# An encoder's Fourier layer, folded by its symmetries

## The chip, the core and the metric

The kernel runs on one core of a Trainium2 chip. Five engines work side by side, each with its own queue of instructions, done in order: TensorE (PE in the profile) multiplies matrices, VectorE (DVE) and ScalarE (ACT) work element by element, GpSimd (POOL) does small things and issues some DMAs, SyncE (SP) issues the others. An instruction waits for others by semaphores, and what stands behind it in its queue waits with it. The metric is the device time of one execution in microseconds (us), and the median over runs.

## The reference

Two layers over 512 positions (S) and 1024 channels (D). Layer 0 is a mixer of attention and a recurrence, layer 1 mixes by a Fourier transform. After each mixer stands a SwiGLU feed-forward network (FFN0, FFN1) with 2816 inner channels. Every part is normed before and after and added to x. The Fourier mixer is:

```python
def fourier_mixer(h, w):
    B, S, D = h.shape
    g = h.astype(jnp.float32).reshape(B, S, FOURIER_GROUPS, FOURIER_GROUP_DIM)
    f = jnp.fft.fft2(g, axes=(1, 3), norm='ortho').real
    return f.reshape(B, S, D).astype(h.dtype) @ w

# one layer
x = x + rmsnorm(mixer(rmsnorm(x, g_mix_pre)), g_mix_post)
x = x + rmsnorm(swiglu(rmsnorm(x, g_ffn_pre)), g_ffn_post)
```

Four groups of 256 channels are transformed on their own, over positions and channels, and the real part goes through a 1024x1024 map w_fourier_out.

## The kernel before

**Number format.** Every operand of a product is split into a rounded high part (hi) and the rest (lo), `split`: ACT casts hi, DVE subtracts it from the source for lo. A product is three matmuls, hi by hi, hi by lo and lo by hi (`mm3`, L108 to L111). A matmul has 128 rows of weights, 128 columns of weights and up to 512 columns of moving data.

**Weights** are streamed. `units` lists blocks of 256 rows or columns in the order of use; `prep_half` (L165) loads half a unit, 128x1024, into one of three raw buffers (NRAW = 3) by a DMA on SP and splits it into two tiles of a pool of 33 tiles of 128x1024 (`tiles`). A raw buffer is free again when its lo subtraction is done. `next_unit(ahead)` (L190) hands out the next unit and prepares some units ahead. The tile pool also holds the feed-forward's gated tiles, the transform's matrices and most intermediate values, so a tile's first writer waits for the last reader of what stood there. PSUM has 8 banks of 128x512.

**Stages** in program order: layer 0's mixer, FFN0, Fourier stage, FFN1. In the down projections and maps (`proj_tok`, L268) tokens are the rows of the output, in four tiles of 128, and the last input tiles are done token tile by token tile, so that `post_norm` (L256) and the next pre-norm of one tile run beside the matmuls of the next. `turn_x` (L246) transposes a normed token tile by PE and splits it into `hn` (hi and lo for the whole sequence, one buffer each, tags hnhi and hnlo in `hpool`). The `ffn` (L739) works on column tiles of 128 inner channels; the first unit of each FFN is done in two halves of 256 tokens (`col_tiles` with halves), so that it can begin with two token tiles turned, and the turns of the last two are deferred into its first pass.

**The Fourier stage** (L782 to L884). `pre_norm_tok` writes tokens in layer 1's pre-norm, without its gain, straight into the hn buffers: hi by ACT, lo by DVE, and calls it in FFN0's tail. The transform over positions (`pos_dft`, L829) takes 128 channels at a time: four token tiles, three products each, 512 columns of which 257 are the cosines and 255 the sines that a real transform needs: 8 x 4 x 3 = 96 matmuls. The gain is multiplied in as u is taken from PSUM (L836, by columns of `vcols`). The transform over channels (`ch_dft`, L848) makes the 256 outputs of a group in two tiles: 8 x 2 x 6 = 96 matmuls of 258 or 256 columns. `mirror` (L861) adds and subtracts cosine and sine part, and so gets tokens 0 to 256 and, reversed, 257 to 511. The map is `proj_tok` over 8 channel tiles, 4 token tiles and 2 halves of D: 8 x 4 x 2 x 3 = 192 matmuls of 512 columns, with `fin1` (post-norm, residual, pre-norm) and `turn_x` of each token tile in its tail. `load_dft` (L804) loads the four position tiles on POOL from call 32 of FFN0's hook on. `after1` (L886) writes the output of each token tile, half on SP's and half on ACT's queue.

The order within a queue follows the program text, as a scheduler places it beside the other engines. It is fixed before the kernel runs.

## Time and profile before

| What | Value |
|---|---|
| median of three runs | 1048.28 us |
| the three runs | 1048.87, 1048.28, 1046.87 us |
| the profiled execution's own time | 1047.91 us |
| its span in the trace | 1046.0 us |
| granted TensorE clock, mean | 0.994 |
| first matmul of the position transform, from the span's start | 597.17 us |
| first matmul of FFN1 | 675.81 us |

Times in the trace are counted from the span's start. The span covers the engines' instructions; the execution's own time is 1.9 us longer. Matmuls overlap: a row's duration (0.39 us for 512 columns) is longer than the distance to the next one's start, so a rate is read from starts.

The operands that the sums need besides come in rows of the engines' timelines: start, duration, engine and line, operation, output and inputs, shape, and in brackets how long the engine stood idle before it and whose instruction ended that.

### The profile page before, as it was taken

Reading aid. Unit: us, or ns where it says so; the run is one execution under the profiler, and the core shown is the slowest. Engines: PE = TensorE matmul, PEld = TensorE weight load, DVE = VectorE, ACT = ScalarE, POOL = GpSimd, SP = SyncE. Lnnn points to the kernel's source line nnn. Section 1 sums busy time; section 2 is a strip of 40 time slices with the busy share of each in tenths; the row PEclk is TensorE's granted clock in tenths of the full one; section 3 lists DMA queues with packets and bytes.
Section 4 is the critical chain, followed back from the end, with each engine's and each line's share of the span. In section 5 each row is a group of like instructions: output and inputs, shape, how many; then the busy total and the mean of one; then the engine's idle time right before and its main releaser. Section 6 shows DMA issues by size and latency. Waiting matters only on the chain.

```text
span 1046.0 us, 12311 instructions
## 1 busy us (share of the span) xinstructions
PE 1030.3 (99%) x4959; PEld 857.9 (82%) x4959; DVE 479.3 (46%) x735; ACT 381.9 (37%) x629; POOL 68.2 (7%) x82
## 2 busy tenths in 40 slices
PE   8999998999999999999999999999999999999997
PEld 7887776789888888888888888898888888888885
DVE  6869988664532222323333555644232232234304
ACT  5378567634432112322322454334211132233202
POOL 1056010110000000000100100100000000000000
PEclk8999999999999999999999999999999999999999
DMA  6434213403734322232442023026432223224002
GB/s 224 125 95 151 67 41 102 141 1 95 224 90 134 103 81 81 93 109 81 142 155 66 21 81 122 17 85 201 124 118 81 81 81 124 78 81 141 1 1 81
DMA packets 72981, 102.41 MB, mean 98 GB/s; under 512 B 3878, under 2 KB 61275, under 8 KB 72924
## 3 DMA queue, kind: packets, MB, share of 16 engines
q1 hardware_dynamic: 69722, 92.44, 28.5%
q0 software_dynamic: 2624, 8.13, 2.4%
q10 hardware_dynamic: 578, 1.05, 0.3%
q8 instruction: 39, 0.64, 0.3%
q14 instruction: 18, 0.15, 0.0%
HBM read 99.51 MB, written 2.10 MB: 97 GB/s over the span
## 4 chain that ended last, share of the span: by engine, by line
PE 89%; DVE 7%; ACT 2%; issue 1%; DMA 1%; POOL 1%; SPq 0%; DVEq 0%; POOLq 0%; ACTq 0%
PE pc L109 15%; PE pc L110 15%; PE pc L111 15%; PE pj L111 10%; PE pj L110 10%; PE pj L109 10%; DVE p L582 2%; DVE wlo L106 1%; DVE p L588 1%; PE pv L111 1%; PE pT L251 1%; PE pv L110 1%; PE pv L109 1%; DVE aT L106 1%; PE pqk L109 1%
## 5 line engine op out<-in xcount | busy, mean ns | idle before, releaser
L106 DVE TENSOR_TENSOR wlo<-raw,whi 128x1024 fp32r<-128x1024 f32 x170 | 206.7, 1239 | 271.2 <-ACT whi L103 220.1
L110 PE MATMUL pc<-hnlo,whi 128*128 128x512 f32 (+1 forms) x768 | 285.1, 372 | 0.0
L109 PE MATMUL pc<-hnhi,whi 128*128 128x512 f32 (+1 forms) x768 | 284.6, 372 | 0.5 <-ACT hnhi L103 0.5
L111 PE MATMUL pc<-hnhi,wlo 128*128 128x512 f32 (+1 forms) x768 | 284.9, 371 | 0.0
L103 ACT CAST whi<-raw 128x1024 fp32r<-128x1024 f32 x164 | 167.7, 1049 | 118.1 <-PE pj L110 31.0
L110 PEld LDWEIGHTS pc<-hnlo,whi 128*128 128x128 f32 x768 | 144.7, 188 | 25.5 <-DVE hnlo L106 0.4
L109 PEld LDWEIGHTS pc<-hnhi,whi 128*128 128x128 f32 x768 | 144.2, 188 | 25.7 <-ACT hnhi L103 1.0
L111 PEld LDWEIGHTS pc<-hnhi,wlo 128*128 128x128 f32 x768 | 144.6, 188 | 25.0
L109 PE MATMUL pj<-whi,gs 128*128 128x512 f32 x352 | 136.9, 389 | 0.0
L110 PE MATMUL pj<-wlo,gs 128*128 128x512 f32 x352 | 136.9, 389 | 0.0
L111 PE MATMUL pj<-whi,gs 128*128 128x512 f32 x352 | 136.9, 389 | 0.0
L93 ACT ACTIVATE gated<-pc 128x512 f32<-128x512 f32 x44 | 26.2, 597 | 271.6 <-PE pc L111 271.6
L749 DVE TENSOR_TENSOR gated<-gated,pc 128x512 f32<-128x512 f32 x44 | 30.2, 686 | 112.8 <-PE pc L111 112.8
L109 PEld LDWEIGHTS pj<-whi,gs 128*128 128x128 f32 x352 | 66.1, 188 | 13.8
L110 PEld LDWEIGHTS pj<-wlo,gs 128*128 128x128 f32 x352 | 66.1, 188 | 13.8
L111 PEld LDWEIGHTS pj<-whi,gs 128*128 128x128 f32 x352 | 66.1, 188 | 13.5
L262 ACT ACTIVATE junk<-pj 128x512 f32<-128x512 f32 x32 | 19.2, 599 | 94.8 <-DVE y L261 57.7
L217 POOL TENSOR_TENSOR r<-m,mhalf 128x1 f32<-128x1 f32 x32 | 17.5, 546 | 543.3 <-DVE m L216 536.8
L261 DVE TENSOR_TENSOR y<-pj,gpost 128x512 f32<-128x512 f32 x32 | 21.9, 688 | 56.6 <-PE pj L111 56.5
L103 ACT CAST gs<-gated 128x512 fp32r<-128x512 f32 x44 | 25.3, 618 | 52.1 <-PE pj L110 32.2
L106 DVE TENSOR_TENSOR gs<-gated,gs 128x512 fp32r<-128x512 f32 x44 | 28.4, 686 | 31.3 <-ACT gs L103 31.3
L93 ACT ACTIVATE p<-p,mn 128x512 f32<-128x512 f32 x32 | 23.0, 720 | 25.8 <-DVE mn L582 24.3
(192 smaller groups left out, 1221.9 us busy)
## 6 DMA issues: line engine op xcount, KB each, us to landing
raw<-in_w_ffn_gate_dram SPq DMA_DIRECT2D x44, 512.0 KB, 4.1
raw<-in_w_ffn_up_dram SPq DMA_DIRECT2D x44, 512.0 KB, 4.8
raw<-in_w_ffn_down_dram SPq DMA_DIRECT2D x44, 512.0 KB, 3.7
raw<-in_w_in_dram SPq DMA_DIRECT2D x20, 512.0 KB, 4.6
raw<-in_w_mix_out_dram SPq DMA_DIRECT2D x8, 512.0 KB, 3.4
raw<-in_w_fourier_out_dram SPq DMA_DIRECT2D x8, 512.0 KB, 3.8
pos<-in_dft_pos_dram POOLq DMA_DIRECT2D x8, 256.0 KB, 5.7
bias<-in_alibi_dram POOLq DMA_DIRECT2D x4, 448.0 KB, 5.3
```

The source lines that it names most:

```text
L93: ins = A.activation(out_, in_, func, **kw)
L103: A.copy(hi, src)
L106: lo_eng.tensor_tensor(out=lo, in0=src, in1=f(hi), op=ALU.subtract)
L109: T.matmul(ps, lhsT=l[0], rhs=r[0], start=start, stop=False)
L110: T.matmul(ps, lhsT=l[0], rhs=r[1], start=False, stop=False)
L111: T.matmul(ps, lhsT=l[1], rhs=r[0], start=False, stop=stop)
L217: G.tensor_tensor(out=r, in0=m, in1=mhalf[:, 0:1], op=ALU.pow)
L251: T.transpose(pt[:, k * P:(k + 1) * P], xh[:, k * P:(k + 1) * P], ident)
L261: V.tensor_tensor(out=ys[h], in0=ps[h], in1=g[:, h * S:(h + 1) * S], op=ALU.mult)
L262: A.activation(junk, ps[h], AF.Square, scale=RD, accum_out=ss[h])
L582: last_score[0] = V.tensor_tensor_reduce(out=pr[m], in0=ps[m], in1=bias[h][:, 384 - t * P:384 - t * P + S], op0=ALU.add, op1=ALU.min, scal ...
L749: V.tensor_tensor(out=gated[fc], in0=gated[fc], in1=ps, op=ALU.mult)
```

## The change

The transform is folded by its symmetries. Cosines over a group's 256 channels are even about channel 128, sines odd. So the pre-norm multiplies by the gain first (h), then adds and subtracts the mirrored channels (j and 256 - j): w holds four groups of 128 sums, with channel 0 in place, and four of 128 differences. `pos_dft` computes the cosines of the sums (258 columns) and the sines of the differences (256): 4 groups x 4 token tiles x 2 x 3 matmuls. Channel 128 of every group is gathered apart by `pos_rest`, 12 matmuls of 258 columns with every fourth column as weights. `ch_dft` needs only output channels 0 to 127: 4 groups x 8 matmuls, and `ch_rest` makes output channel 128 of every group, the rest's rows and the sums for token 256, in 10.

Since outputs k and 256 - k of a group have the same even part and the opposite odd part, the map's rows are folded too: `fold_w` loads rows j (SP) and 256 - j (an indirect DMA on POOL), adds and subtracts on DVE, and writes both back to a DRAM tensor `wfold` (POOL), one group after each of FFN0's units 0 to 3. The map's four units are loaded from there; `last_unit` keeps the prefetch from reaching them until FFN0 is through. The lo parts of the first two (units 48 and 49, LO_POOL) are subtracted on POOL instead of DVE.

The even part `fe` and the odd part `fo` of the transform, and the rows beside them, stand in the hn buffers (`feo`, `rows_`), where the normed tokens stood. The map runs over 256 positions in two halves i = 1 and i = 0 of 128, even and odd into banks of their own: 96 matmuls and 8 more of `map_rest`. Token 256 needs sums over channels by e256 (DVE: four tiles of wfold loaded again, times a column each, added up in `acc`, and split). `map_out` takes difference and sum of the two: tokens t and 512 - t, then the norms. The token tiles 1 and 2 are in reversed order from here on: their x comes by indirect gathers from a DRAM copy `scratch` that SP wrote in FFN0's tail, and goes to the output by indirect scatters on POOL in `after1`. `row_index` makes the index columns on POOL at the kernel's start (eight of iota and memset each).

Both token tiles of i = 1 are turned after the whole map. The other two are deferred into FFN1's first pass, which covers the first three weight units (six column tiles) in halves, and two more column tiles in whole width from then on (`wide`). `load_ch` builds the small channel matrices on POOL, mostly by memsets and one-column DMAs, at hook call 8; the position matrices come in pieces with a few POOL instructions each.

```diff
-LO_POOL = ()
+LO_POOL = (48, 49)
...
-        units.append(unit_rows(w_fourier_out, u * 256))
+        units.append(unit_rows(wfold, u * 256))
...
+    def fold_w(g):
+        a, b, c = (tile1k("fold") for _ in range(3))
+        nc.sync.dma_start(a, w_fourier_out[g * 256:g * 256 + P, :])
+        gather(b, w_fourier_out, rowx["w%d" % g])
+        G.memset(b[0:1, :], 0.0)
+        V.tensor_tensor(out=c, in0=a, in1=b, op=ALU.add)
+        V.tensor_tensor(out=a, in0=a, in1=b, op=ALU.subtract)
+        for z, w in enumerate((c, a)):
+            G.dma_start(wfold[g * 256 + z * P:g * 256 + (z + 1) * P, :], w)
...
-        while emitted[0] <= i + ahead and emitted[0] < len(units):
+        while emitted[0] <= i + ahead and emitted[0] < last_unit[0]:
...
-                    if deferred and (h == 1 or c == P):
+                    if deferred and (h == 1 or c == P) and not (late and h == 0):
                         deferred.pop(0)()
+                while late and deferred:
+                    deferred.pop(0)()
...
+            ug, uu, vg = next_unit(2), next_unit(1), next_unit(0)
+            col_tiles([(ug, 0), (ug, P), (uu, 0), (uu, P), (vg, 0), (vg, P)],
+                      lambda i, ps: consume(i, ps, 0) if i < 4 else consume(i - 4, ps, 1), True, True)
+            vu = next_unit(3)
+            col_tiles([(vu, 0), (vu, P)], lambda i, ps: consume(i + 2, ps, 1), False)
...
+        h = tile1k("h")
+        V.tensor_tensor(out=h, in0=xt[t], in1=g_pre1[0], op=ALU.mult)
+        hv = h.rearrange("p (g c) -> p g c", c=256)
+        w = tile1k("w")
+        wv = w.rearrange("p (z g c) -> p z g c", g=4, c=P)
+        V.tensor_copy(wv[:, :, :, 0:1].rearrange("p z g c -> p g (z c)"), hv[:, :, 0:256:P])
+        V.tensor_tensor(out=wv[:, 0, :, 1:P], in0=hv[:, :, 1:P], in1=hv[:, :, 255:P:-1], op=ALU.add)
+        V.tensor_tensor(out=wv[:, 1, :, 1:P], in0=hv[:, :, 1:P], in1=hv[:, :, 255:P:-1], op=ALU.subtract)
         hi = hn["hi"][:, 2 * t:2 * t + 2, :].rearrange("p a b -> p (a b)")
         lo = hn["lo"][:, 2 * t:2 * t + 2, :].rearrange("p a b -> p (a b)")
+        for z in range(2):
+            sl = slice(z * S, (z + 1) * S)
+            A.activation(hi[:, sl], w[:, sl], AF.Copy, scale=r)
+            V.scalar_tensor_tensor(out=lo[:, sl], in0=w[:, sl], scalar=r, in1=f(hi[:, sl]), op0=ALU.mult, op1=ALU.subtract)
...
+        if t >= 2:
+            nc.sync.dma_start(scratch[(t - 2) * P:(t - 1) * P, :], xt[t])
...
+        w128 = tile1k("w128")
+        G.memset(w128, 0.0)
+        for q in range(3):
+            G.dma_start(w128[32 * q:32 * q + 4, :], w_fourier_out.rearrange("(g j) d -> g j d", j=256)[:, P, :])
...
+                G.dma_start(w[:, 0:257], dft_pos[z, k * P:(k + 1) * P, 0:257])
+                G.dma_start(w[:, 258:513], dft_pos[z, k * P:(k + 1) * P, 257:512])
+                G.memset(f(w[:, 257:258]), 0.0)
...
+    ffn(0, after0, 6, load_dft, early=lambda u: fold_w(u - 1) if 0 < u < 5 else None)
+    last_unit[0] = len(units)
+    load_last()
+    prep_one()
...
+            for z, (r0, o0, n) in enumerate(((0, 0, 258), (257, 256, 256))):
+                o = (z * 4 + g) * P
+                mm3(ps[:, o0:o0 + n], [a[:, o:o + P] for a in hf[t]], [a[:, r0:r0 + n] for a in posT[t]],
+                    t == 0 and z == 0, t == 3 and z == 1, skip_group_check=True)
...
+            mm3(ps[:, 0:258], [a[:, S:2 * S:4] for a in hf[t]],
+                [a[:, 0:258] for a in posT[t]], t == 0, t == 3)
...
+    for g in range(4):
+        pos_dft(g, (0, 1, 2))
+    pos_rest((0, 1, 2))
+    pos_rest((3,))
+    uts["r"] = pair("u", F32R)
+    split(*[a[:, 0:258] for a in uts["r"]], ups["r"][:, 0:258])
+    for g in range(4):
+        pos_dft(g, (3,))
+        take_u(g)
...
+    feo = hpool.tile([P, 16, 256], F32R, name=nm("feo"), tag="hnhi")
+    rows_ = hpool.tile([P, 4, D], F32R, name=nm("rows"), tag="hnlo")
+    acch, accl, wr, fr = rows_[:, 0, :], rows_[:, 1, :], rows_[:, 2, :], rows_[:, 3, 0:256]
...
+        ut, ur = uts[g], uts["r"]
+        mm3(pe[:, 0:258], (chw(0), chw(1)), [a[:, 0:258] for a in ut], True, False)
+        for a in ur:
+            T.matmul(pe[:, 0:258], lhsT=chw(4 + g), rhs=a[:, 0:258], start=False, stop=a is ur[1])
+        mm3(po[:, 0:256], (chw(2), chw(3)), [a[:, 256:512] for a in ut], True, True)
+        eo = feo[:, 4 * g:4 * g + 4, :]
+        e, o = fe[g], fo[g] = (eo[:, 0, :], eo[:, 1, :]), (eo[:, 2, :], eo[:, 3, :])
+        split(*e, pe[:, 0:256])
...
+        A.copy(wr, w128)
+        V.tensor_tensor(out=wr[32:64, :], in0=w128[32:64, :], in1=f(wr[32:64, :]), op=ALU.subtract)
...
+    gather(xr[1], scratch, rowx["d"])
+    gather(xr[2], scratch, rowx["c"])
...
+    for g in range(4):
+        raw = raws.tile([P, 1024], F32, name=nm("raw"), tag="raw")
+        nc.sync.dma_start(raw, wfold[g * 256:g * 256 + P, :])
+        if g:
+            V.scalar_tensor_tensor(out=acc, in0=raw, scalar=e256[g], in1=acc, op0=ALU.mult, op1=ALU.add)
+        else:
+            V.tensor_scalar(out=acc, in0=raw, scalar1=e256[0], scalar2=None, op0=ALU.mult)
+    V.scalar_tensor_tensor(out=acc[0:32, :], in0=w128[0:32, :], scalar=e256["r"][0:32, :], in1=acc[0:32, :], op0=ALU.mult, op1=ALU.add)
+    split(acch, accl, acc)
...
+        ps = psm[i]
+        mm3(ps[0][h], [a[:, sl] for a in fe[g]], [a[:, d] for a in wf[g][0]], g == 0, False)
+        mm3(ps[1][h], [a[:, sl] for a in fo[g]], [a[:, d] for a in wf[g][1]], g == 0, g == 3 and i == 1)
...
+        for h in range(2):
+            A.copy(ts[h], psm[i][1][h])
+        for z in (0, 1) if i else (1, 0):
+            for h in range(2):
+                V.tensor_tensor(out=ys[h], in0=psm[i][0][h], in1=ts[h], op=ALU.add if z else ALU.subtract)
+            t = (3 - z, z)[i]
+            post_norm(t, ys, g_post1)
+            pre_norm(t, g_fpre1)
+            ys = ts
...
+    for i in (1, 0):
+        for g in range(4):
+            for h in range(2):
+                map_part(i, h, g)
+        for h in range(2):
+            map_rest(i, h)
+        prep_one()
+        if i == 0:
+            new_hn()
+            turn_x(0)
+            turn_x(1)
+        map_out(i)
+    deferred.extend((lambda: turn_x(2), lambda: turn_x(3)))
...
+        if t in (1, 2):
+            G.indirect_dma_start(out=out, out_offset=rowx[("od", "oc")[t - 1]], in_=xt[t], in_offset=None)
+            return
...
-    ffn(1, after1, 4)
+            q.dma_start(out[r:r + P, h * S:(h + 1) * S], xt[t][:, h * S:(h + 1) * S])
+    ffn(1, after1, 4, wide=True)
```

Three places in the queues show where the change moves instructions. On POOL, from the end of FFN0's tail on, r is the root of a norm, ch the channel matrices, w_810 the tile with row 128 of each group of the map (w128), x_817 and x_818 the reversed token tiles. Before:

```order
L217 TENSOR_TENSOR r_4750<-m_4749,mhalf 128x1
L819 DMA ch_4769<-in_dft_ch_dram 128x1024
L217 TENSOR_TENSOR r_4763<-m_4762,mhalf 128x1
L819 DMA ch_4771<-in_dft_ch_dram 128x1024
L217 TENSOR_TENSOR r_5232<-m_5231,mhalf 128x1
```

And now:

```order
L251 TENSOR_TENSOR r_4910<-m_4909,mhalf 128x1
L888 MEMSET w_810_4925 128x1024
L199 DMA x_817_4942<-scratch,ixd 128x1024
L890 DMA w_810_4925<-in_w_fourier_out_dram 4x1024 x3
L107 TENSOR_TENSOR wlo_4933<-raw_4930,whi_4932 128x1024
L987 MEMSET feo_5084 128x1 x8
L199 DMA x_818_4943<-scratch,ixc 128x1024
L107 TENSOR_TENSOR wlo_4939<-raw_4936,whi_4938 128x1024
L107 TENSOR_TENSOR wlo_5075<-raw_5072,whi_5074 128x1024
L107 TENSOR_TENSOR wlo_5081<-raw_5078,whi_5080 128x1024
L251 TENSOR_TENSOR r_5306<-m_5305,mhalf 128x1
```

Between the last root of FFN0 and the first of the Fourier stage POOL had one channel matrix to load; now a memset, two gathers, three DMAs, eight small memsets and four lo subtractions stand there. These four are called A, B, C and D below, and the gathers d and c.

On ACT, at the start of the Fourier stage, put is a bank of the position transform, u its split value. Before:

```order
L788 ACTIVATE hnhi_4562<-x_82,r_4763 128x1024
L836 ACTIVATE u_4836<-put_4773,vcols 128x512
L836 ACTIVATE u_4842<-put_4783,vcols 128x512
L836 ACTIVATE u_4848<-put_4793,vcols 128x512
L836 ACTIVATE u_4854<-put_4803,vcols 128x512
```

And now:

```order
L846 ACTIVATE hnhi_4688<-w_4916,r_4910 128x512 x2
L104 CAST whi_4938<-raw_4936 128x1024
L991 CAST rows_5085<-w_810_4925 128x1024
L104 CAST u_5033<-put_5020 128x258
L104 CAST u_5042<-put_4944 128x512
L104 CAST u_5051<-put_4963 128x512
```

The first cast of u stood right behind the last token; the cast of a weight and that of these rows 128, which come by POOL's DMAs, stand between them now.

On DVE, from the last map weights to the first norm behind the map, y is a half of a token tile on its way to the post-norm, pj and pm are the map's banks. Before:

```order
L106 TENSOR_TENSOR wlo_5166<-raw_5163,whi_5165 128x1024
L106 TENSOR_TENSOR wlo_5172<-raw_5169,whi_5171 128x1024
L106 TENSOR_TENSOR wlo_5184<-raw_5181,whi_5183 128x1024
L106 TENSOR_TENSOR wlo_5190<-raw_5187,whi_5189 128x1024
L261 TENSOR_TENSOR y_5223<-pj_5107,gpost_5101 128x512
```

And now:

```order
L107 TENSOR_TENSOR wlo_5196<-raw_5193,whi_5195 128x1024
L1002 TENSOR_TENSOR rows_5085<-pe_5160,rows_5085 64x256
L107 TENSOR_TENSOR wlo_5202<-raw_5199,whi_5201 128x1024
L1029 TENSOR_SCALAR acc_5205<-raw_5206,e_839_5098 128x1024
L1027 SCALAR_TENSOR_TENSOR acc_5205<-raw_5209,e_842_5116,acc_5205 128x1024
L1027 SCALAR_TENSOR_TENSOR acc_5205<-raw_5212,e_845_5134,acc_5205 128x1024
L1027 SCALAR_TENSOR_TENSOR acc_5205<-raw_5215,e_848_5152,acc_5205 128x1024
L1030 SCALAR_TENSOR_TENSOR acc_5205<-w_810_4925,e_850_5171,acc_5205 32x1024
L107 TENSOR_TENSOR wlo_5282<-raw_5279,whi_5281 128x1024
L107 TENSOR_TENSOR rows_5085<-acc_5205,rows_5085 128x1024
L107 TENSOR_TENSOR wlo_5288<-raw_5285,whi_5287 128x1024
L1057 TENSOR_TENSOR y_5292<-pm_5225,yt_5291 128x512
```

The first value that DVE takes from a map bank stood behind four lo subtractions; it now also stands behind the four products with re-loaded tiles (raw_5206 to raw_5215) and acc's split, with FFN1's first weights (wlo_5282, wlo_5288) between them.

201 lines of the change are left out of this document (125 added, 76 removed).

## The prediction

> **What bounds the kernel now.** I read the page from its top: span, busy times, and the chain of work that ended last.
>
> ```profile
> span 1046.0 us, 12311 instructions
> PE 1030.3 (99%) x4959; PEld 857.9 (82%) x4959; DVE 479.3 (46%) x735; ACT 381.9 (37%) x629; POOL 68.2 (7%) x82
> PE 89%; DVE 7%; ACT 2%; issue 1%; DMA 1%; POOL 1%; SPq 0%; DVEq 0%; POOLq 0%; ACTq 0%
> ```
>
> PE carries 89% of the chain, so on the whole fewer matmuls mean less time. The change shortens one stage, and that stage is what counts. The PE timeline gives its borders (start, duration, instruction), and the view by windows its rate.
>
> ```profile
> 597.17 0.39 PE L109 MATMUL put<-pos,hnhi 128*128 128x512 f32 x1
> ...
> 613.49 0.28 PE L109 MATMUL pe<-u,ch 128*128 128x258 f32 x1
> ...
> 630.48 0.40 PE L109 MATMUL pj<-whi,f 128*128 128x512 f32 x1
> ...
> 675.81 0.28 PE L109 MATMUL pc<-hnhi,whi 128*128 128x256 f32 x1
> ...
> 689.46 0.74 PE L109 MATMUL pc<-hnhi,whi 128*128 128x256 f32 x4 [0.24 <-ACT hnhi L103]
> ```
> ```profile
> core 0: us, PE busy (x) PEld busy (x) DVE busy (x) ACT busy (x) POOL busy (x), PEclk, DMA share, GB/s
> 597.17:613.49 16.32, 16.32 (x74) 13.51 (x72) 6.40 (x12) 6.43 (x12) 2.76 (x5) 1.00 0.30 97
> 613.49:616.36 2.87, 2.87 (x26) 2.87 (x24) 2.47 (x5) 2.01 (x5) 0.00 (x0) 1.00 0.00 0
> 630.48:647.06 16.58, 16.58 (x76) 13.71 (x75) 10.30 (x16) 8.05 (x14) 0.00 (x0) 1.00 0.57 178
> ```
>
> The Fourier stage runs from the first position matmul (597.17, called t = 0 from here on) to FFN1's first matmul (675.81): 78.64 us. In its first two windows PE is busy all the time at a granted clock of 1.00. The weight loads count the matmuls that started: 72 of 512 columns in 16.32 us, **0.227 us** each; 24 of 256 or 258 in 2.87 us, **0.120 us** each. So a matmul of half the columns costs about half, and cutting columns pays. No other engine is near its limit here: DVE is busy 10.30 of the 16.58 us of the last window.
>
> **PE's own gain.** Before, the stage has 96 position and 192 map matmuls of 512 columns (288 x 0.227 = 65.3 us), 96 channel matmuls of half size (11.5) and 16 transposes (1.6): 78.4, against 78.64 in the trace. After, it has 96 + 12 position, 32 + 10 channel matmuls of half size (150 x 0.120 = 18.0) and 104 of the map (23.6): 41.6 us without transposes. PE drops some 35 us of work. FFN1 then turns two more column tiles to halves: 96 x 0.120 = 11.5 instead of 48 x 0.227 = 10.9, **+0.6 us**. The weight fold, the token fold and the gathers lie on DVE, SP and POOL, outside PE.
>
> **What is late next.** What used to hide under 78 us of PE must now fit under 42, in the order that the queues have been given. I added durations of rows along these queues.
>
> The first two rows give shortest, median and longest of eight, in ns; the others count, busy time and mean of a group, and then size and median landing of a DMA.
>
> ```profile
> L494 POOL TENSOR_TENSOR gate<-gate,xc x8: 1287/1296/2266, 59.9 to 74.6; 128x512 f32<-128x512 f32 x8
> L520 POOL TENSOR_TENSOR gate<-gate,th x8: 1282/1785/2917, 86.4 to 99.8; 128x512 f32<-128x512 f32 x8
> ```
> ```profile
> L819 POOL DMA_DIRECT2D ch<-in_dft_ch_dram x2 | 1.1, 572 | 0.0
> ...
> masks.py:197 POOL MEMSET ident<- 128x128 f32 x1 | 0.2, 204 | 0.3 <-POOLq L935 0.3
> ```
> ```profile
> L106 DVE TENSOR_TENSOR wlo<-raw,whi 128x1024 fp32r<-128x1024 f32 x170 | 206.7, 1239 | 271.2 <-ACT whi L103 220.1
> ...
> L103 ACT CAST whi<-raw 128x1024 fp32r<-128x1024 f32 x164 | 167.7, 1049 | 118.1 <-PE pj L110 31.0
> ...
> raw<-in_w_fourier_out_dram SPq DMA_DIRECT2D x8, 512.0 KB, 3.8
> ```
> ```profile
> raw<-in_w_ffn_gate_dram SPq DMA_DIRECT2D x44, 512.0 KB, 4.1
> ...
> out_dram<-x SPq DMA_DIRECT2D x4, 256.0 KB, 2.0
> ```
>
> *POOL queue.* At t = 6.8 it is through with the last token's root and a vector load; SP's write of the last token tile to the scratch, issued at 4.4, lands a microsecond later. Then come a memset of 128x1024 (about 1.0, an estimate between the 0.204 of 128x128 and eight times it), the gather of token tile d, three small DMAs (3 x 0.57), and the lo subtraction A; eight tiny memsets (0.3); the gather of c; the subtractions B, C and D, each 128x1024. No row shows a gather's issue: a plain DMA takes 0.57 of POOL, the longest POOL instruction of the page's groups here is 2.92. I take 1.3 for each, nearer to the plain DMA, which moves the same 512 KB; the upper end, 5.8, is that longest row doubled for 128x1024. A subtraction of 128x512 takes 1.29 at best, 1.79 in the median of the crowded group, 2.92 at worst, so 128x1024 lies between 2.6 and 5.8. I take **2.9**, near twice the uncrowded row, since most of DVE's work at this time reads one operand from PSUM. POOL then ends D at 6.8 + 1.0 + 1.3 + 1.7 + 0.3 + 1.3 + 4 x 2.9 = **24.0**.
>
> [...]
>
> *Raw buffers.* There are three, so the load of a raw tile waits for the lo subtraction three tiles back. D frees the buffer that the first half of the last map unit waits for: issued 24.1, landed 27.9 (3.8), cast 1.05, lo 1.24: 30.2. The four re-loads of folded tiles for acc go through the same buffers: the second can be issued only at 30.3 and lands at 34.1; three products and the 32-row one follow (34.1 + 4 x 1.3 = 39.4). FFN1's first weights stand behind them: loaded at 39.5, cast to 40.6, lo 41.9; acc's lo 43.0, another weight's lo **44.2**. Only then does DVE's queue reach the differences of map half 1, whose banks PE finished at about 34.
>
> *Token chain.* One token of post-norm and pre-norm:
>
> ```profile
> 649.75 0.69 DVE L261 TENSOR_TENSOR y<-pj,gpost 128x512 f32<-128x512 f32 x1 [3.39 <-PE pj L111]
> 651.50 0.56 POOL L217 TENSOR_TENSOR r<-m,mhalf 128x1 f32<-128x1 f32 x1 [48.17 <-DVE m L216]
> 652.10 1.42 DVE L266 SCALAR_TENSOR_TENSOR x<-y,r,x 128x512 f32<-128x512 f32 x2 [0.69 <-POOL r L217]
> ...
> 655.20 1.41 DVE L243 SCALAR_TENSOR_TENSOR xn<-x,r,gpre 128x512 f32<-128x512 f32 x2
> ```
>
> 649.75 to 656.61 is 6.9 us. With two differences ahead (1.4) the first token is done at 44.2 + 1.4 + 6.9, about 52.7; the second, with two weights' lo subtractions queued between, 7.6 later at 60.3. PE turns it, ACT casts it (0.54), and FFN1's first matmul starts at **60.9**. PE needs its map until about 46.5 (it starts the map at 21.0 and loses 1.4 to a bank that a cast in ACT's queue frees late), so 14 us of idle PE are left before FFN1. Against 78.64 this is **-17.7 us**: half of what PE saves. From D's end to FFN1 it is 36.9 us in single file; a microsecond on POOL is a microsecond of the end.
>
> *Start of the stage.* ACT's queue has the cast of the map's rows 128 (w128) ahead of every u cast. Their DMAs stand behind the gather (the last issued at 10.3 and landed at 12.6: 2.3, a little over the 2.0 of 256 KB), so the cast ends at 14.2 and the first channel matmul waits from 13.0 to 15.0, with 1.0 more behind DVE's lo of these rows. These 3 us lie within the 60.9 and add nothing to it.
>
> *FFN0's tail.* The 33-tile pool now also holds two channel tiles, h and w there, so weight casts wait for PE to let tiles go. A wait of this kind shows cast and lo (1.05 + 1.24) less six matmuls (1.36), 0.93; I count three of them, **+2.8 us**, between 0 (the tiles come free in time) and 5.
>
> *FFN1's start.* Its first pass now covers six column tiles, whose third unit's weights are cast behind the token chain, and the last two turns come together.
>
> ```profile
> 688.82 1.08 ACT L103 CAST hnhi<-pT 128x512 fp32r<-128x512 f32 x2 [5.54 <-PE pT L251]
> 689.44 1.29 DVE L106 TENSOR_TENSOR hnlo<-pT,hnhi 128x512 fp32r<-128x512 f32 x2 [5.23 <-ACT hnhi L103]
> ```
>
> Before, PE lost 0.24 and a second gap of about 0.5 here. Now PE has nothing beside four pairs of these pieces: 1.0 until the first hi, 0.8 until the last lo, and 1.6 for the third unit: 3.4, so **+2.6 us** (0 if the tokens are early, 5 if they are late).
>
> *The end.* Token tiles 1 and 2 go out by POOL scatter, and the last plain output waits for them.
>
> ```profile
> 1035.22 0.54 POOL L217 TENSOR_TENSOR r<-m,mhalf 128x1 f32<-128x1 f32 x1 [4.89 <-DVE m L216]
> 1040.66 0.54 POOL L217 TENSOR_TENSOR r<-m,mhalf 128x1 f32<-128x1 f32 x1 [4.90 <-DVE m L216]
> ...
> 1041.24 1.41 DVE L266 SCALAR_TENSOR_TENSOR x<-y,r,x 128x512 f32<-128x512 f32 x2 [0.72 <-POOL r L217]
> ...
> 1042.68 0.34 ACTq L888 DMA_DIRECT2D out_dram<-x  x1
> ```
>
> The scatter of tile 2 starts at about 1035.22 + 0.54 + 0.06 + 1.41 + 0.7 = 1037.9; with 1.3 of issue and a landing of 4.1 as for other 512 KB it is done at 1043.3, past the 1042.68 at which the last write was issued: **+1 us** (0.5 to 2).
>
> **The sum**: -17.7 + 0.6 + 2.8 + 2.6 + 1.0 = -10.7. The profiled execution's own time is 1047.91 (0.37 below the median of the three runs), so 1037.2; I round to **1038**.
>
> **The rivals.**
> *More of the gain arrives.* If subtractions take 2.6 (1.2 saved in all), gathers 0.57 (1.5) and the three loads in the single file 3.3 each (1.5), and the FFN0 term is 0 (2.8), the net is -10.7 - 7.0 = -17.7. A stage bound by PE alone would give -35 + 0.6, and some 6 back for the last token's chain: -28. Between the two, about 1026 (1020 to 1032). For it speaks that DVE and ACT have room (46% and 37%); against it the three raw buffers.
> *POOL and DVE get in each other's way.* With 5.1 per subtraction (4 x 2.2 = +9) the net is about -2: 1046. The 2917 in the gate row speaks for it, the median of 1296 against it. In this case the work on POOL takes back nearly everything.
> *Slower: the gathers hold POOL.* If an indirect DMA of 128 rows takes G of POOL's time, the two in the middle cost 2 x (G - 1.3), since everything behind D is in single file; at the end the scatter of tile 2 stands ahead of the last token's root, which it delays from G = 2.8 on, and the landing moves by G - 1.3 too. G = 3 gives 5.4 in all (-5), G = 5 gives 7.4 + 6.0 = 13.4, so +2.7: **1050.5**. It turns the sign at about 4.3. The 0.57 of plain DMAs speaks against it; that no indirect DMA is in the trace leaves it open.
> *The half-size matmuls don't get cheap* (strided weights, sums of mixed widths in one bank): 150 at 0.227 instead of 0.120 is +16 of PE, and with none of it under waits -10.7 + 16 = +5.3, 1053. The second window speaks against it.
>
> **How the numbers follow.** The forecast (1033 to 1044) gets 0.54, more of the gain 0.18, POOL against DVE 0.13, the gathers 0.11, full-price matmuls 0.04. The range goes from 1026, half of the gain's case, to 1049, past the contention and its edge: 0.54 + 0.09 + 0.13 + 0.04 from the gathers' lower half, 0.80. This kernel's measurements tell differences from about 0.2% (2.1 us) on. Slower by that (over 1050.4) takes most of the gathers' and the full-price cases, 0.13; within it the edges of both and of the contention, 0.08; faster 0.79.
>
> **What would show it.** PE's timeline: 41 to 43 us of matmul time from the first position matmul to the last of the map, and an idle stretch of 10 to 18 us before FFN1's first matmul, which starts 57 to 64 us after t = 0. POOL: four subtractions of 2.6 to 3.5, gathers of 1 to 2. The chain: DVE, SP's loads and POOL in the stage instead of PE. Waits of raw loads ended by POOL. I am wrong if that idle stretch is under 5 us, if a gather or a subtraction is above 4, or if FFN0's end moves by more than 5.

## The result and the profile after

| | before | after |
|---|---|---|
| median of four runs | 1047.82 us (1046.87 to 1048.87) | **1040.60 us** (1040.22 to 1042.30) |
| ratio after to before, with its 95% interval | | 0.9934 (0.9917 to 0.9951) |
| the profiled execution's own time | 1047.91 us | 1040.47 us |
| its span | 1046.0 us | 1038.7 us |

The kernel is 7.2 us faster, where some 10 were forecast (the terms add up to -10.7, the time was rounded up), and the time lies in the range. The page of the kernel after, from the lines that were shown of before:

```profile
span 1038.7 us, 12339 instructions
PE 1004.3 (97%) x4877; PEld 836.9 (81%) x4877; DVE 497.4 (48%) x761; ACT 377.8 (36%) x621; POOL 123.7 (12%) x200
PE 77%; DVE 11%; issue 4%; POOL 3%; ACT 3%; DMA 2%; DVEq 0%; POOLq 0%; ACTq 0%
```

PE works 26 us less (1030.3 to 1004.3), and its share of the chain falls from 89% to 77%: what it no longer does was replaced in the chain, for the greater part, by DVE, POOL and DMA. The PE timeline of the kernel after (start, duration, instruction, idle time ahead and what ended it) has the borders of the terms, and what is new among its waits:

```profile
531.98 0.50 PE L110 MATMUL pj<-whi,gs 128*128 128x512 f32 x1 [0.48 <-ACT gs L104]
544.20 0.50 PE L110 MATMUL pj<-whi,gs 128*128 128x512 f32 x1 [1.02 <-ACT gs L104]
556.03 0.50 PE L110 MATMUL pj<-whi,gs 128*128 128x512 f32 x1 [0.48 <-ACT gs L104]
...
616.98 0.39 PE L110 MATMUL pe<-u,ch 128*128 128x258 f32 x1 [2.56 <-ACT u L104]
...
619.88 0.58 PE L110 MATMUL po<-u,ch 128*128 128x256 f32 x1 [2.03 <-DVE u L107]
...
627.37 0.40 PE L110 MATMUL pm<-whi,feo 128*128 128x512 f32 x1
...
654.27 1.29 PE L285 MATMUL pT<-ident,xn 128*128 128x128 f32 x8 [3.11 <-DVE xn L277]
661.78 1.97 PE L285 MATMUL pT<-ident,xn 128*128 128x128 f32 x8 [6.22 <-DVE xn L277]
663.57 1.01 PE L110 MATMUL pc<-hnhi,whi 128*128 128x256 f32 x3
```

The first position matmul (t = 0) starts at 599.71, the map's first at 27.7 and its last pair at 50.8 from there, and FFN1's first matmul at 663.57, which is t = 63.86. PE idles 3.11 and then 6.22 us for the token chain (DVE's xn), and the eight transposes that follow take 1.29 and 1.97 us. The same borders in both traces measure the terms of the sum:

| Term | forecast | before | after | measured |
|---|---|---|---|---|
| FFN0's tail: start of t = 0 | +2.8 | 597.17 | 599.71 | +2.54 |
| stage: t = 0 to FFN1's first matmul | -17.7 | 78.64 | 63.86 | **-14.78** |
| FFN1's first to last matmul (the +0.6 and +2.6) | +3.2 | 362.60 | 365.97 | +3.37 |
| last matmul's start to the span's end | +1.0 | 7.59 | 9.16 | +1.57 |
| sum | -10.7 | 1046.0 | 1038.7 | -7.30 |

Only one term is off by more than a microsecond; that some of the others came right by luck is said further down. The chain of waits in the stage (start, duration, engine or DMA) shows where it went; the rows are those from the last two subtractions on POOL to the first difference, without the pieces of under half a microsecond:

```profile
619.41 4.72 POOL wlo L107 x2
624.14 4.21 DMA raw<-wfold
628.38 1.06 ACT whi L104
629.46 1.24 DVE wlo L107
630.71 3.94 DMA raw<-wfold
634.75 1.30 DVE acc L1027
636.06 5.00 DMA raw<-in_w_ffn_gate_dram
641.44 1.06 ACT whi L104
642.53 1.19 DVE wlo L107
643.71 1.07 DVE rows L107
646.05 1.29 DVE y L1057 x2
```

This is the single file that the prediction drew up, in its order: D on POOL, the raw buffer it frees, the last map weights, the second re-load for acc, FFN1's first weights, acc's split, the difference. D ended at 624.12 (t = 24.4; 24.0 forecast). The three loads took 4.21 + 3.94 + 5.00 = 13.15 us where the prediction had 3.8 for each of the first two and, by its times, 4.1 for the third (issued behind the product at 34.1 + 1.3, loaded at 39.5). The first difference came at t = 46.3 instead of 44.2. What POOL's instructions cost (count and shape, busy time, mean in ns, idle time ahead), grouped from t = 0 on to the map's middle:

```profile
L107 POOL TENSOR_TENSOR wlo<-raw,whi 128x1024 fp32r<-128x1024 f32 x4 | 9.5, 2384 | 1.2 <-ACT whi L104 1.1
...
L199 POOL DMA_INDIRECT x<-scratch,ixd x1 | 1.4, 1412 | 0.2 <-issue 0.2
L199 POOL DMA_INDIRECT x<-scratch,ixc x1 | 1.0, 1019 | 0.2 <-issue 0.2
```

A gather holds POOL for 1.41 and 1.02 us (1.3 forecast), so the rival in which it takes over 4 falls. A subtraction takes 2.38 (2.9 forecast), so 4 x 0.5 were gained there. They were given back, and 0.4 more: POOL idles 1.1 us ahead of C for a cast that stands behind u's casts in ACT's queue, and the last token's root, ahead of all this, ends at t = 8.2 instead of 6.8.

### The profile page after: what moved, and what is told of

It is laid out like the page before. It is cut to its first block, busy times and chain, and to the rows that moved or that the text cites. A ratio compares the mean times of both kernels' runs of the same rounds, so it can differ in the third digit from the quotient of the medians.

```text
span 1038.7 us, 12339 instructions
## 1 busy us (share of the span) xinstructions
PE 1004.3 (97%) x4877; PEld 836.9 (81%) x4877; DVE 497.4 (48%) x761; ACT 377.8 (36%) x621; POOL 123.7 (12%) x200
## 4 chain that ended last, share of the span: by engine, by line
PE 77%; DVE 11%; issue 4%; POOL 3%; ACT 3%; DMA 2%; DVEq 0%; POOLq 0%; ACTq 0%
PE pc L110 15%; PE pc L112 15%; PE pc L111 15%; PE pj L110 8%; PE pj L112 8%; PE pj L111 8%; DVE wlo L107 2%; DVE p L617 2%; DVE p L623 1%; DVE x L300 1%; POOL wlo L107 1%; DMA raw<-wfold 1%; POOL r L251 1%; DVE aT L107 1%; PE pqk L110 1%
## 5 line engine op out<-in xcount | busy, mean ns | idle before, releaser
L107 DVE TENSOR_TENSOR wlo<-raw,whi 128x1024 fp32r<-128x1024 f32 x166 | 202.2, 1240 | 233.7 <-ACT whi L104 182.2
L110 PE MATMUL pc<-hnhi,whi 128*128 128x512 f32 (+1 forms) x784 | 288.2, 369 | 1.0 <-ACT hnhi L104 1.0
L112 PE MATMUL pc<-hnhi,wlo 128*128 128x512 f32 (+1 forms) x784 | 288.3, 368 | 0.5 <-DVE wlo L107 0.5
L111 PE MATMUL pc<-hnlo,whi 128*128 128x512 f32 (+1 forms) x784 | 288.4, 368 | 0.0
L112 PEld LDWEIGHTS pc<-hnhi,wlo 128*128 128x128 f32 x784 | 148.3, 189 | 25.5 <-DVE wlo L107 1.0
L110 PEld LDWEIGHTS pc<-hnhi,whi 128*128 128x128 f32 x784 | 148.0, 189 | 25.8 <-ACT hnhi L104 1.7
L111 PEld LDWEIGHTS pc<-hnlo,whi 128*128 128x128 f32 x784 | 148.3, 189 | 24.6 <-DVE hnlo L107 0.2
L111 PEld LDWEIGHTS pj<-wlo,gs 128*128 128x128 f32 x352 | 66.1, 188 | 13.7
L296 ACT ACTIVATE junk<-pj 128x512 f32<-128x512 f32 x24 | 14.3, 597 | 74.5 <-DVE y L295 53.4
L295 DVE TENSOR_TENSOR y<-pj,gpost 128x512 f32<-128x512 f32 x24 | 16.4, 687 | 48.1 <-PE pj L112 48.1
```

What stands on the lines that cost most here:

```text
L107: lo_eng.tensor_tensor(out=lo, in0=src, in1=f(hi), op=ALU.subtract)
L110: T.matmul(ps, lhsT=l[0], rhs=r[0], start=start, stop=False, **kw)
L111: T.matmul(ps, lhsT=l[0], rhs=r[1], start=False, stop=False, **kw)
L112: T.matmul(ps, lhsT=l[1], rhs=r[0], start=False, stop=stop, **kw)
L295: V.tensor_tensor(out=ys[h], in0=ps[h], in1=g[:, h * S:(h + 1) * S], op=ALU.mult)
L296: A.activation(junk, ps[h], AF.Square, scale=RD, accum_out=ss[h])
```

## The experiments

Each is the kernel after with one edit, unless said otherwise, and each ratio is to the kernel before. The theory was the prediction's, corrected by the trace: the end is set by the single file, POOL's subtractions and the four re-loads. Against it stood the start of the stage (casts in ACT's order), the low clock (0.50 in after from 619.88 to 625.37 us), the tile pool and the outputs.

### Without the sums for token 256 (e1)

```diff
-    acc = tile1k("acc")
-    for g in range(4):
-        raw = raws.tile([P, 1024], F32, name=nm("raw"), tag="raw")
-        nc.sync.dma_start(raw, wfold[g * 256:g * 256 + P, :])
...
-    split(acch, accl, acc)
...
-            for a in (acch, accl):
-                T.matmul(psm[i][1][h], lhsT=chw(13), rhs=a[:, d], start=False, stop=a is accl)
+            T.matmul(psm[i][1][h], lhsT=chw(13), rhs=wr[:, d], start=False, stop=True)
```

It leaves out the sums of the four groups for token 256.

> Leaves out the sums for token 256 from the four folded groups (the four re-loads of wfold, the products on DVE and acc's split); the two matmuls that added acc are one with the w128 rows. Single-file theory: DVE's queue reaches the first difference of map half 1 when PE is through with that half and ACT has copied two banks, about 40.4 us after the first position matmul instead of 46.3; the 17.5 us from there to FFN1's first matmul stay: FFN1 starts at 58 instead of 63.9, the time is about 1034.6. Rival (PE's late start and its low clock set the end): the time falls by less than 2 us.

1035.94 us, ratio 0.9891 (0.9875 to 0.9908): 4.7 us faster than after. FFN1's first matmul comes at t = 55.38, 8.5 us earlier, so the products and re-loads were in the file; but FFN1 then takes 368.76, 2.8 more than after. Two waits on its PE timeline that after does not have:

```profile
656.85 1.18 PE L110 MATMUL pc<-hnhi,whi 128*128 128x256 f32 x3 [0.69 <-DVE hnlo L107]
...
671.63 0.39 PE L110 MATMUL pc<-hnhi,whi 128*128 128x256 f32 x1 [1.31 <-ACT whi L104]
```

PE waits for the lo part of the turned tokens and for the hi part of a weight: when the stage is shorter, the next things that are late are FFN1's tokens and weights.

### The sums on PE (e2)

Token 256's row is made by matmuls with one column of weights, 26 in all, in the map's second half, so that nothing is loaded again.

```diff
-        e256[g] = sm("e256")
-        V.tensor_copy(e256[g], pe[:, 256:257])
+        e256[g] = [small.tile([P, 1], F32R, name=nm("e256"), tag="e%d" % i, bufs=5) for i in range(2)]
+        split(*e256[g], pe[:, 256:257])
...
+            for g in range(4):
+                mm3(row, e256[g], [a[:, d] for a in wf[g][0]], False, False, skip_group_check=True)
+            T.matmul(row, lhsT=e256["r"], rhs=wr[:, d], start=False, stop=False, skip_group_check=True)
```

> The same sums for token 256 by 26 matmuls with one weight column each on PE, in place of re-loads, products and split. Single-file theory: PE works 5.9 - 0.9 = 5 us longer in a stretch where it was idle for over 10, its map ends at about 56, DVE's file is 6 us shorter: FFN1 starts at 58 to 59, the time is about 1035.5. Rival (PE is what the stage waits for): 5 us of PE work cost up to 5, 1041 to 1045.

1036.23 us, ratio 0.9896 (0.9879 to 0.9912): 4.4 us faster. The map's last matmul comes at t = 55.7 instead of 50.8, later by the new matmuls, and still FFN1 starts at 58.44, 5.4 earlier. PE has no idle stretch left between map and FFN1 that is longer than 0.4 us. Against e1, which has neither the re-loads nor these matmuls, FFN1 starts 3.1 later but then takes 366.24 instead of 368.76, so in the time the added matmuls cost 0.3 us, which is within the runs' spread.

### The lo parts back on DVE (e3)

```diff
-LO_POOL = (48, 49)
+LO_POOL = ()
```

> The four lo subtractions A to D on DVE instead of POOL. Single-file theory: DVE idles from 610.1 to 616.2 in the trace and takes 1.24 for each instead of 2.38, so D is done some 4 us earlier and the chain behind it (load, cast, lo, re-load) moves with it; DVE gets 5 us more work, most of it before: FFN1 starts 3 us earlier (1 to 5), the time is about 1037.5. Rival (DVE is the bound of the stage and the move to POOL is what makes the gain): slower by 2 to 5, 1043 to 1046.

1037.97 us, ratio 0.9915 (0.9898 to 0.9931): 2.6 us faster. FFN1 starts at t = 58.62 (-5.2) and takes 367.62 (+1.65). A subtraction takes 1.24 on DVE, which stood idle in after for 6.05 us ahead of 616.19, and 2.38 on POOL behind gathers and waits. The two waits at the start of the stage go too (the map begins at t = 20.5 instead of 27.7), but e4, below, shows that this alone is worth nothing. This part of the change costs time.

### The casts of u ahead of the rows' cast (e4)

```diff
+        u_casts.append(A.copy(uts[g][0], ups[g]))
...
-        A.copy(wr, w128)
+        order_after(A.copy(wr, w128), u_casts)
```

> The cast of the w128 rows is ordered behind the casts of u on ACT. Single-file theory: the two waits of 2.6 and 2.0 us before the channel matmuls go, PE's clock stays full there and the channel stage ends some 7 us earlier, but only the 1.1 us that POOL waits for a cast lies in the file: FFN1 starts 1 us earlier (0 to 2), the time is about 1039.5. Rival (PE's late start and its low clock set the end): 4 to 7 us faster, 1034 to 1036.5.

1040.80 us, ratio 0.9937 (0.9920 to 0.9953): nothing gained. Yet the start of the stage is as it was meant. Windows of this kernel (start and end, length, busy time of PE, weight loads, DVE, ACT, POOL, clock, DMA share, GB/s):

```profile
599.95:614.50 14.55, 14.55 (x110) 14.55 (x109) 9.45 (x18) 8.46 (x17) 8.96 (x10) 1.00 0.45 149
614.50:618.00 3.50, 3.50 (x32) 3.50 (x31) 1.90 (x5) 1.84 (x4) 3.33 (x11) 1.00 0.69 183
```

PE goes from the position into the channel matmuls without a wait, at a clock of 1.00, and the map begins at t = 20.1 instead of 27.7. FFN1 begins at 64.02 all the same. D ends at t = 23.3, 1.1 us earlier, but the chain of this kernel goes from C, at t = 21.0, through a raw load of 6.44 us, and has its first difference at t = 46.4 as after has at 46.3. The 1 us that was expected did not come. So the 7.5 us at the start lay beside the file, as the prediction had it of its 3 us.

### Channel matrices late, and plain outputs (e5)

```diff
-        if calls[0] == 8:
+        if calls[0] == 31:
             load_ch()
...
-            G.indirect_dma_start(out=out, out_offset=rowx[("od", "oc")[t - 1]], in_=xt[t], in_offset=None)
-            return
-        r = (P, None, None, 0)[t]
+        r = (P, 3 * P, 2 * P, 0)[t]
```

Rows of the output of two token tiles stay in reversed order.

> Two edits at two places that the trace keeps apart. The channel matrices are loaded at hook call 31 instead of 8, so two tiles of the pool come free in FFN0's down projection; and token tiles 1 and 2 are written by plain DMAs (in reversed order of rows, so the output differs there). Tile theory: the three waits of PE for a gs cast (0.5, 1.0, 0.5) go and the first position matmul starts at 597.2 to 597.7 instead of 599.7. End theory: from the last matmul to the end of the span 7.6 us instead of 9.2. Together 3.5 us: about 1037. Rivals: the waits come from the fold's work on DVE and POOL, then 599.7 stays; the end is that of the last plain write, then 9.2 stays.

1039.89 us, ratio 0.9935 (0.9918 to 0.9952). FFN0's three waits are still 0.48, 1.02 and 0.48, so it isn't the time at which the channel matrices take their tiles. The end takes 8.92 instead of 9.16: the scatters aren't the 1.57 us. Neither of the two theories held.

### PE kept busy ahead of the turns (e6)

```diff
-            turn_x(0)
-            turn_x(1)
+            for n, t in ((13, 0), (26, 1)):
+                w_ = bank("pT")
+                for _ in range(n):
+                    T.matmul(w_, lhsT=chw(0), rhs=wf[0][0][0][:, 0:S], start=True, stop=True)
+                turn_x(t)
```

> 39 more matmuls of 512 columns into the banks of the transposes, 13 before the first turn and 26 before the second, where PE is idle: they are overwritten, and only keep PE busy. Single-file theory: the transposes and the first FFN1 matmuls run at full clock, but PE waits less early and more later, for the third unit's weights and the last tokens: FFN1 starts up to 1 us earlier, the time changes by less than 1, 1040 to 1041. Clock rival: the two slow stretches cost what they show, 0.9 in the transposes and 1.3 in FFN1's first 22 us: 1038.4.

1043.96 us, ratio 0.9970 (0.9959 to 0.9982): 3.4 us slower than after, which neither forecast had. Its PE timeline at the turns:

```profile
655.17 1.03 PE L285 MATMUL pT<-ident,xn 128*128 128x128 f32 x8
...
661.96 1.03 PE L285 MATMUL pT<-ident,xn 128*128 128x128 f32 x8
...
666.21 0.74 PE L110 MATMUL pc<-hnhi,whi 128*128 128x256 f32 x4 [3.22 <-ACT hnhi L104]
```

The transposes take less now (1.03 instead of 1.29 and 1.97; the granted clock is 1.00 from 651 to 664 us, where after has 0.71 from 650.90 to 663.57), and the second set is 1.2 us earlier counted from t = 0. But then ACT's cast is late, by 3.22 us: it stands behind a piece of the next token's norm in ACT's queue here, and ahead of it in after. And t = 0 itself is 1.35 later than in after, which it already was when FFN0's down projection began (478.01 against 476.68), far ahead of the edit. Whether the clock alone is worth anything can't be read from this run: it moved the wait and the start together.

### FFN1's first pass as before (e7)

```diff
-    ffn(1, after1, 4, wide=True)
+    ffn(1, after1, 4)
```

> FFN1's first pass covers one unit pair (four column tiles) in halves as before, with the turns of the last two tokens inside it. Theory: the last tokens are ready only at about 674 and 680, so PE waits for them twice, some 4 us in all, and saves 0.6 of half-size matmuls and the wait for the third unit: 2 to 4 us slower, 1042.5 to 1044.5. Rival (the wide pass costs the 2.6 us that the forecast gave it): 1 to 3 us faster, 1037.5 to 1039.5.

1040.26 us, ratio 0.9936 (0.9919 to 0.9952). FFN1 takes 366.00 against 365.97, and neither of the two forecasts came. Of the 4 us of waits for the last tokens the timeline shows 1.10 and 0.24. The pass over six column tiles neither costs nor saves in the balance: what FFN1 loses, it loses with the old pass as well. The +0.6 and +2.6 of the sum came out right together, but not as the price of that pass.

### The three of e2, e3 and e4 together (e8)

The row for token 256 on PE, the lo parts on DVE and the casts of u first.

> The row for token 256 on PE, the lo subtractions on DVE and the w128 cast behind the casts of u, together. Theory: with the file gone, map half 1 is taken as PE finishes it (about 32.5 after the first position matmul), 17.5 us later FFN1 starts at 50 to 53 instead of 63.9; 3 to 4 us of that are given back in FFN1's first pass to weights and tokens that are late: about 1032 (1030 to 1034). Rival (two of the three shorten the same wait, so the gains don't add): no better than the best alone, 1035 to 1036.5.

**1031.01 us**, ratio 0.9847 (0.9830 to 0.9863): 9.6 us faster than after, more than the 4.4, 2.6 and 0 of the three alone, and faster than both kernels. The PE timeline around the end of its map:

```profile
649.66 1.91 PE L285 MATMUL pT<-ident,xn 128*128 128x128 f32 x16
651.91 0.50 PE L110 MATMUL pc<-hnhi,whi 128*128 128x256 f32 x2 [0.34 <-ACT hnhi L104]
...
653.68 0.39 PE L110 MATMUL pc<-hnhi,whi 128*128 128x256 f32 x1 [1.27 <-DVE hnlo L107]
```

FFN1 starts at t = 51.96, 0.34 us after the turns, and PE was busy for 50.9 of the 52 us. The file is gone; PE bounds the stage again. FFN1 takes 368.25, so 2.3 us of what the stage wins are lost there.

### The fold in two other buffers (e9), the prefetch free (e11)

Both start from e8, and both were to find what FFN0 waits for. e9 takes the fold's three tiles out of the pool of 33 (the first two lines below); e11 lets the prefetch reach the map's units in FFN0 (the last).

```diff
-        a, b, c = (tile1k("fold") for _ in range(3))
+        a, b = (xpool.tile([P, D], F32, name=nm("fold"), tag="x2" if z else "x3") for z in range(2))
...
-    last_unit[0] = len(units) - 4 - NF // 2 * 3
```

> e8 with the fold's tiles taken from the two buffers that later hold the reversed tokens, not from the pool: a + b replaces b, and 2a - (a + b) replaces a. Rotation theory: the pool hands out its 33 buffers in turn, and the twelve tiles of the fold shift which buffer a weight or gs tile gets; without them the three waits of PE for gs in FFN0 (0.5, 1.0, 0.5) go, the first position matmul starts at 597.3 instead of 599.9 and the time is 1028.6. Rival (the waits come from the fold's work on DVE, POOL and SP): 599.5 to 600.5, and 1031.

> e8 without the line that keeps the prefetch from the map's units until FFN0 is through: four halves of them are loaded and cast in FFN0's tail, as in the kernel before. Hold-back theory: the three waits of PE for gs in FFN0 come from the order that this line makes, they go, the first position matmul starts at 597.5 to 598 instead of 600, and the time is 1028 to 1029.5. Rival (the waits come from which pool buffers are taken, and the map's first weights were not waited for): 599.5 to 600.5, and within 1 us of 1031.

e9: 1069.14 us, ratio 1.0211 (1.0197 to 1.0225), which neither forecast had. The two buffers are those of token tiles 2 and 3, which FFN0 still uses, so the whole fold moved behind FFN0's tail. The trace shows it there:

```profile
632.02 0.58 PE L110 MATMUL pe<-u,ch 128*128 128x258 f32 x1 [12.69 <-ACT u L953]
```

FFN1 starts at t = 89.99, 38.0 us later than in e8. So much does the fold of the weights cost when it runs behind FFN0, with two buffers and one group after another. FFN0's three waits are 0.48, 1.02 and 0.48 in this kernel too, without any fold beside them.

e11: 1040.19 us, ratio 0.9931 (0.9914 to 0.9947), 9.2 slower than e8, and FFN0's waits unchanged once more. Its DVE timeline at the start of FFN0's tail:

```profile
579.06 1.23 DVE L107 TENSOR_TENSOR wlo<-raw,whi 128x1024 fp32r<-128x1024 f32 x1 [7.33 <-issue]
580.20 2.49 DVE L107 TENSOR_TENSOR gs<-gated,gs 128x512 fp32r<-128x512 f32 x4
583.63 0.69 DVE L295 TENSOR_TENSOR y<-pj,gpost 128x512 f32<-128x512 f32 x1 [0.94 <-PE pj L112]
```

SP issued seven loads of the map's weights by 580.6 (in e8 three by 557.1 and the next at 608.9), and their lo subtractions stand among FFN0's last pieces (gs): the first y of the tail comes at 583.63, in e8 at 571.58. The last normed tokens are late, and the position transform waits 2.75 and 1.96 us for them (ACT's hnhi). Holding the prefetch back is worth its place.

### What the end waits for (e10, e12)

Two edits of the kernel *before*: e10 adds one indirect gather of 128 rows ahead of FFN0, e12 the DRAM tensor and SP's writes of two token tiles to it.

```diff
+    G.iota(ix, pattern=[[0, 1]], base=256, channel_multiplier=-1)
...
+    G.indirect_dma_start(out=raw, out_offset=None, in_=w_fourier_out, in_offset=bass.IndirectOffsetOnAxis(ap=ix, axis=0))
```
```diff
+        if t >= 2:
+            nc.sync.dma_start(scratch[(t - 2) * P:(t - 1) * P, :], xt[t])
```

> The kernel before with one index column and one indirect gather of 128 rows added ahead of FFN0, into a raw buffer that nothing reads. Theory: a program that uses the indirect DMA on POOL takes longer to close, so the stretch from the last matmul to the span's end grows from 7.6 to 9.1 us, the time by 1.5 to 1049 (with up to 0.5 for the gather's load). Rival (the longer close comes from something else, the larger number of DMAs and DRAM tensors): 7.6 stays and the time stays within 0.5.

> The kernel before with a DRAM scratch tensor and the write of token tiles 2 and 3 to it by SP, as in the change, and nothing that reads it. Theory: a program with tensors of its own in DRAM takes longer to close, the stretch from the last matmul to the span's end grows from 7.6 to 9.1, and the time by 1.5 to 1048.7. Rival (the close depends on something else): 7.6 stays, and the time stays within 0.5.

e10: 1047.41 us, ratio 1.0001 (0.9991 to 1.0010); e12: 1047.01 us, ratio 0.9999 (0.9990 to 1.0009). From the last matmul's start to the end they take 7.61 and 7.45, as before (7.59). Neither the indirect gather nor the DRAM tensor lengthened the end here.

## Why the prediction was right, and where it was off

**The stage (-17.7, measured -14.8): mechanism right, size off by 2.9.** The step "D frees the buffer ... landed 27.9 (3.8)" and the two loads after it were priced with medians of the kernel before, 3.8 for the old map's loads and 4.1 for the FFN's. (A small slip beside it: 44.2 + 1.4 + 6.9 is 52.5, not 52.7.) Windows of the kernel after:

```profile
599.71:608.51 8.80, 8.80 (x73) 8.79 (x72) 6.26 (x13) 4.62 (x11) 3.39 (x5) 1.00 0.42 149
608.51:611.33 2.82, 2.82 (x15) 2.82 (x14) 1.41 (x2) 1.74 (x3) 2.64 (x4) 1.00 0.41 112
...
619.88:625.37 5.49, 5.47 (x24) 5.18 (x25) 4.56 (x11) 3.30 (x8) 4.24 (x2) 0.50 0.59 185
627.37:650.90 23.53, 23.53 (x106) 19.34 (x104) 18.42 (x24) 8.32 (x14) 0.57 (x1) 1.00 0.73 222
650.90:663.57 12.67, 3.31 (x19) 2.41 (x17) 11.07 (x22) 8.55 (x20) 1.66 (x3) 0.71 0.18 50
```

While PE does the map, the DMA engines are busy for 0.73 of the time at 222 GB/s; before, in the map's window that the prediction shows, it was 0.57 at 178. That this traffic made the loads longer is argued: no run changed it alone. The loads' 13.15 instead of 11.7 are 1.45 us of the error, of which the third load has 0.9; D's end is 0.4, and the casts and subtractions behind the third load 0.3. The rest, 0.8, lies between the first difference and FFN1, the greater part of it in the last turn: 1.2 us from its normed token to FFN1's first matmul where 0.6 was drawn, in a window whose mean clock was 0.71. That the file sets FFN1's start is shown from both sides: shorten it (e1, e2, e3) and FFN1 starts 5 to 8.5 us earlier; win 7.5 us beside it (e4) and nothing moves. The gain of PE time went where the forecast said, into a chain over POOL, three raw buffers, SP and DVE; e8 takes the chain apart and gets 11.9 us more out of the stage (51.96 against 63.86), of which 9.6 arrive.

**PE's own work** was drawn too small. Its busy time in the stage fell from 78.64 to 49.88, by 28.8 us instead of 35, and from the first position matmul to the end of the map it was 46.8 where 41 to 43 were named as a sign. The stretch at half clock (5.5 us), the transposes (1.29 + 1.97 instead of 1.6) and 12 matmuls with strided weights (below) make up most of the difference. PE's idle time ahead of FFN1, 3.11 + 6.22 us, is just under the 10 to 18 that were named; FFN1's start, at 63.86, is inside the 57 to 64.

**"Subtractions of 2.9" and "gathers of 1.3"** were near: 2.38, and 1.41 and 1.02. The first is below the 2.6 to 3.5 that were named as a sign. The prediction took 2.9, near the lower end of its 2.6 to 5.8, because DVE's work there mostly reads one operand from PSUM; that this keeps a subtraction on POOL short was the author's assumption, which no row of before shows. In after A takes 2.40 us while DVE idles, B 2.38 beside the rows' subtraction, and C and D 4.72 together while DVE subtracts from PSUM banks (u and feo): the four differ by little, whatever DVE does. What the prediction didn't draw is that POOL would wait for ACT between them. Pieces that took longer while the other engine worked were there, a large one on DVE (below) that lay beside the file, and a small one on POOL at its head: the last token's root took 1.05 us, while DVE added and subtracted the mirrored channels (w). The three other roots of FFN0's tail that run beside such pieces took 0.93, 0.86 and 0.86, the other four 0.55 to 0.57.

```profile
606.88 1.05 POOL L251 TENSOR_TENSOR r<-m,mhalf 128x1 f32<-128x1 f32 x1
```
```profile
606.23 0.68 DVE L840 TENSOR_TENSOR w<-h 128x508 f32<-128x508 f32 x1
606.83 0.68 DVE L841 TENSOR_TENSOR w<-h 128x508 f32<-128x508 f32 x1
```

By an estimate from these rows that cost the file up to 0.5 us.

**"The half-size matmuls don't get cheap"** got 0.04 as a rival against all 150, and is true of 12. The first window above has 72 weight loads in 8.80 us, 0.122 each; the second only those of `pos_rest`, whose weights are every fourth column, 12 in 2.82 us, 0.235 each; one such weight load takes 0.33 us where the others take 0.19. The 12 matmuls cost 1.4 us more, beside the file.

**"Start of the stage"**: 3 us of waits were drawn, 2.56 + 2.03 came, and a clock of 0.50 behind them. The cast of the rows 128 ended at t = 16.5 instead of 14.2 (by the prediction's own rows 12.6 + 1.05 is 13.7). That all this adds nothing was right (e4).

**FFN0's tail (+2.8, measured +2.54)**: three waits were counted and three came, of 0.48, 1.02 and 0.48, each behind a cast of weights on ACT that itself waited for PE to let a tile go, as the prediction drew it:

```profile
530.17 1.05 ACT L104 CAST whi<-raw 128x1024 fp32r<-128x1024 f32 x1 [8.07 <-PE pj L112]
...
541.63 2.00 ACT L104 CAST whi<-raw 128x1024 fp32r<-128x1024 f32 x2 [9.19 <-PE pj L111]
...
554.23 1.05 ACT L104 CAST whi<-raw 128x1024 fp32r<-128x1024 f32 x1 [6.86 <-PE pj L112]
```

But such casts wait in the kernel before too (7.83, 5.37 and 7.42 us near these times), and PE doesn't wait behind them there. That the tiles added by the change make the difference isn't supported: another time of the channel matrices (e5), no fold beside it (e9) and a free prefetch (e11) left all three as they were. Why they come only now stays open. The size was near in part by luck: FFN0's down projection, from its first matmul to t = 0, takes 123.03 instead of 119.68, 3.35 more, but began 0.81 earlier (476.68 against 477.49). That beginning differs between kernels that are alike up to there (478.01 in e6, 476.63 in e5).

**FFN1's start (+3.2, measured +3.37)**: right in size, by luck, since it isn't the price of the six-tile pass (e7). What is seen are late tokens and weights, and a low clock: in after PE waits 0.73 us for tokens and 0.46 for a weight's lo (before: 0.24 for tokens), and FFN1's first 2.6 us ran at a granted clock of 0.50. When the stage ends earlier, weights are waited for longer (e1).

**The end (+1.0, measured +1.57)**: the step "the last plain output waits for them" failed. The second scatter was issued at 1028.67 and landed 3.4 us later, by about 1032.1, where the prediction gave it 1.3 + 4.1; the last x was done at 1033.82, and ACT's queue issued the last output right behind it:

```profile
1033.86 0.34 ACTq L1084 DMA_DIRECT2D out_dram<-x  x1
```

From there to the span's end it is 4.84 us, before 1046.0 - 1042.68 = 3.32. Without the scatters it is still 4.63 (e5), and with a gather or a DRAM tensor in the kernel before still 3.33 (e10) and 3.17 (e12). What makes it longer is open, so that the size was near is luck. Combinations of the three weren't tried.

## What to carry to other kernels

When matmuls are taken out of a stage, draw up the chain of everything that they used to cover, queue by queue, and price it against the work that is left; here a saving of 35 us of PE work, as it was drawn, became 15 us of time in the stage. Then look at what stands in that chain only because another engine seemed busy: work moved to a slower engine, or data loaded again to spare PE, may belong on the engine that now waits (e2 and e3, and e8 with both; a subtraction of 128x1024 took 2.38 us on POOL and 1.24 on DVE). Price a load in such a chain for the stretch that it will run in: here three loads took 13.15 us where medians gave 11.7.
